# One decoder layer (gated linear attention and a convolutional FFN): FFN operand blocks moved to multiples of 256 bytes, bank evictions given an earlier place in the issue order, and side work placed on other units

## The chip, the cores and the metric

The kernel runs on one core of one Trainium2 chip. The metric is the device time of one execution in microseconds (us). Three timed executions of the kernel before took 2171.86, 2174.41 and 2174.84 us; their median, 2174.41 us, is the time before. A separate, profiled execution of the same kernel gave the trace that is read below.

## The reference, cut to what matters

One layer, sequence 2048, model width 1024, FFN width 2816, all in f32.

```python
def post_norm_residual(x, cs, w_mod, b_mod, ln_gain, ln_bias, sublayer):
    shift, scale, gate = jnp.split((cs @ w_mod + b_mod)[:, None, :], 3, axis=-1)
    y = sublayer(x * (1 + scale) + shift)
    return layer_norm(DN_ALPHA * x + (1 + gate) * y, ln_gain, ln_bias)

def gla_mixer(h, ...):                      # 4 heads, chunks of 64 tokens
    q, k, v, r, a_lr = split(h @ w_in)
    log_a = log_sigmoid(a_lr @ w_a2 + b_a) / 16      # the decays
    q_dec, k_inv, k_dec = q * exp(cumsum), k * exp(-cumsum), k * exp(last - cumsum)
    o = (causal part inside the chunk) + (state carried from chunk to chunk)
    return (rms_norm(o) * norm_g * silu(r)) @ w_o

def conv_ffn(h, w_up, conv_w, conv_b, w_down):
    u, g = split(h @ w_up)
    u = causal_conv_width_3(u) + conv_b
    return (silu(u) * g) @ w_down

x = post_norm_residual(x, ..., gla_mixer)
x = post_norm_residual(x, ..., conv_ffn)
```

## The kernel before, in words

**Products.** Every large product is made of 128x512 matmuls. An f32 operand is split into a rounded high part and a remainder (`split`, L104 on ScalarE and L107 on VectorE), and `mm3` (L110 to L112) issues high by high, high by low and low by high. Where a product has a 2x2 block form, it uses seven products in place of eight (the tuple `PROD` is their order); the sums that this needs are VectorE work.

**Stages, in order of time.** (1) A start with the modulation vectors and the first Q and K products. (2) `v_group(0)`, then `r_group(0)`: V, and R with its silu, for the first half of the tokens. (3) `v_group(1)` and `r_group(1)` for the second half. (4) The attention stage, seven segments of eight units each, in the order Q1, Q2, O0, Q3, O1, O2, O3 (`q_segment` makes Q and K of a block of 512 tokens, `o_segment` the output product of a block with the residual). The sixteen heads (four blocks by four heads) are worked in between. (5) The FFN's up product: 44 iterations (22 column blocks by two token halves) of seven products of 12 matmuls. Products 0, 1, 5 and 4 read their moving operand from tiles of tag `xa`, products 6, 3 and 2 from tiles of tag `xb`. (6) The down product with the last norm.

**Units and ticks.** A weight unit is one 512 KB block of a streamed weight (`unit`, `issue`, `load_unit`): it is loaded, split two units ahead of its use, and used by 24 matmuls. After a unit `tick()` runs the steps that are registered for it with `at_unit(u, f, ...)`. So the order in which side work stands in the program is written by hand as unit numbers: V0, R0, V1, R1, B0 = 0, 14, 34, 48, 68 are the first units of the stages, and B0 + 16, + 32, + 40, + 48 the first units of O0, O1, O2, O3. Side steps that matter here: `decays` (L564 on: a small matmul, then Identity, Abs, Exp, Ln on ScalarE, a scan on VectorE, two Exps; each call loads an activation table first), `x_prep` (loads and modulates x), `head_s`, `head_a`, `head_b`, `head_c`, `head_d` (the steps of a head), `ln1` and `normalise` (the first norm of 128 tokens: statistics on VectorE, the inverse root on GpSimd, the scaling on ScalarE), `ln1_out` (transposes the normed rows on TensorE into PSUM, L1305, and modulates them on VectorE, L1310), `load_z` (loads the rows of x to which O adds, L1319), `part_end` and `x_first` (free the attention tiles and make the FFN's first operands).

**Order on an engine.** All DMAs are issued by SyncE's queue. The framework sorts each engine's instructions at build time by a simulated run: of the instructions that the simulation finds ready, the one with the lowest number goes first, and the number is the place in the program. On the chip each engine then keeps that order. `tc.high_priority(offset=n)` lowers the numbers inside it by n; offset 0 leaves them as they are.

**Banks.** PSUM has two tags of four banks each. The big products use `mm`, the heads, transposes and decays mostly `w`. An eviction is the instruction that reads a finished bank: `keep` (L420, ScalarE) for the partial sums p1, u2 and u3; `qk_out` (L659, L660); the residual sum in `o_segment` (L1351, VectorE), which needs the rows from `load_z`; the product with `sr` in `head_d` (L1271); the split of `KTt` in `head_a`; the state update L1235 and the copy L1256.

**Addresses.** In the FFN stage a pool at the right end of SBUF holds, from the right: 224 bytes of constants, a 4096-byte tile `G`, two `U` tiles and eight `xa` tiles of 8192 bytes. A `U` tile is 1032 f32, 4128 bytes, so two take 8256 = 32*256 + 64 bytes and the `xa` tiles start at 192 modulo 256. The `xb` tiles and the weight tiles `hl` start at 0 modulo 256. In the down product both operands that are named `dhl` lie in `xa` tiles; one in three pairs lies in `hl` tiles.

Of the kernel before, what the change touches and what calls it, by code (L numbers as in the profile page):

```python
# [16 lines left out]
P = 128  # L17
# [21 lines left out]
def kernel(  # L39
# [84 lines left out]
    def load_unit():  # L124
        src = stream[len(stream_loads)][0]
        raw = src() if callable(src) else raw_tile()
        dst = raw if callable(src) or len(src.shape) == 2 else raw.rearrange("p (n x) -> p n x", n=4)
        stream_loads.append(None if callable(src) else load(dst, src))
        loaded.append(raw)

    def issue(n):
        while len(issued) < min(n, len(stream), stop[0]):
            src, keep_in, kept, gate = stream[len(issued)]
# [9 lines left out]
            if gate is not None:  # L143
                rv = raw.rearrange("p (k c) -> p k c", k=2)
                nc.vector.tensor_tensor(rv, rv, gate()[:, None, :].to_broadcast([P, 2, 512]), op=ALU.mult)
# [162 lines left out]
    def u_tile(up, name="U"):  # L308
        return up.tile([P, 1032], F32, tag="U", name=name, bufs=2)
# [69 lines left out]
    def at_unit(u, fn, *a):  # L379
        steps.setdefault(u, []).append((fn, a))  # L380

    def tick():
        u = pos[0]
        pos[0] += 1
        for fn, a in steps.pop(u, []):
            fn(*a)

# [30 lines left out]
    def keep(po, name):  # L418
        t = t2p.tile([P, 512], F32, tag="t2", name=name)
        return t, nc.scalar.copy(t, po)  # L420
# [5 lines left out]
    if True:  # L426
# [8 lines left out]
        h3_pool[0] = evp  # L435
        xrow = x.rearrange("(t p) d -> t p d", p=P)
# [123 lines left out]
        def a3_load(tb):  # L560
            a3[tb] = t2p.tile([P, TB], F32R, tag="t2", name="A3")[0:96]
            load(a3[tb].bitcast(F32), a3_d[tb])

        def decays(tb, heads):  # L564
# [3 lines left out]
            if "u3" in accs:  # L568
                order(ld, accs["u3"])
            A3 = a3.pop(tb)  # L570
            for h in heads:
# [21 lines left out]
                if tb < 2:  # L593
                    store(e_d[tb][h][:, lo], E1)
                    store(e_d[tb][h][:, hi], E2)

# [7 lines left out]
        def evac_a(pa, tb):  # L604
            A3 = t2p.tile([96, TB], F32R, tag="t2", name="A3")
            nc.scalar.copy(A3, pa[0:96])
            nc.vector.tensor_tensor(A3[32:64], pa[32:64], A3[32:64].bitcast(F32), op=ALU.subtract)
            store(a3_d[tb], A3.bitcast(F32))

# [47 lines left out]
        def qk_out(tb, h, pq, pk):  # L657
            t = raw_tile("qk")
            nc.scalar.copy(t[:, 0:512], pq)  # L659
            nc.scalar.copy(t[:, 512:1024], pk)  # L660
            store(qk_d[tb][h], t)

# [170 lines left out]
        def v_group(hf, X):  # L833
# [7 lines left out]
            for i in PROD:  # L841
# [76 lines left out]
        def x_stage1(i):  # L918
            raws = []
            for pr in range(2):  # L920
# [92 lines left out]
        def x_prep(pr):  # L1013
# [13 lines left out]
            store(xt1_d[3][pr], b21)  # L1027

# [18 lines left out]
        for k, f, pr in ((0, t_first, 1), (1, v_sums2, 0), (2, t_6, 0), (3, t_6, 1), (4, v_sums2, 1), (5, t_3, 0), (6, t_3, 1),  # L1047
                         (8, t_2, 0), (9, t_2, 1)):
            at_unit(V0 + k, f, pr)
        at_unit(V0 + 8, r_first, 0)  # L1050
        at_unit(V0 + 11, r_first1)
        at_unit(V0 + 12, r_first2)
        at_unit(V0 + 11, waw_load)
# [4 lines left out]
        at_unit(R0 + 3, x_prep, 0)  # L1058
        at_unit(R0 + 8, x_prep, 1)
# [4 lines left out]
        load(cb_sb, cb)  # L1064
        for n in range(16):
            u = V1 + 2 + n if n < 8 else R1 + n - 5
            at_unit(u, mods, n)
            if n % 4 == 3:
                at_unit(R1 + 2 if n < 8 else u + 2, mod_fin, 1, n // 4)
        at_unit(R1 + 14, mod2)  # L1070
        at_unit(V1 + 9, r_first, 1)
        at_unit(V1 + 11, r_first1)
        at_unit(V1 + 12, r_first2)
        at_unit(V1 + 11, waw_load)
        at_unit(R1, gate_rows, 2, XN1)
        at_unit(R1 + 4, waw_load)
        at_unit(R1 + 6, gate_rows, 3, XN1)
        for k in range(8):
            at_unit(R1 + 6 + k, gate_step, 0, k, gs1)
        at_unit(R1 + 17, gate_end, 0, gs1)  # L1080

        for pr in range(4):
            at_unit(R1 + 16, get_early, pr)
# [27 lines left out]
        def get(key, pr):  # L1111
            kind, tb = key
            t = xg_tile()
# [28 lines left out]
        def head_l(H):  # L1142
            tb, h = H["tb"], H["h"]
            if tb < 2:
                H["E"] = ab.tile([P, 2, 512], F32, tag="E", name="E")
                load(H["E"], e_d[tb][h].rearrange("p (s c) -> p s c", s=2))
            H["qk"] = ab.tile([P, 2, 512], F32, tag="qk", name="qk")
# [40 lines left out]
        def head_a(H):  # L1188
# [4 lines left out]
            split(KTt[:, 0], KTt[:, 1], pt)  # L1193
# [18 lines left out]
        def head_b(H):  # L1212
            h, v, KTt, el = H["h"], H["v"], H["KT"], H["el"]
            H["S"] = []
            for g in range(2):
# [9 lines left out]
                for i in range(2):  # L1225
# [6 lines left out]
                    if H["S"][s] is None:  # L1232
                        nc.vector.tensor_copy(new, po)
                    else:
                        nc.vector.scalar_tensor_tensor(new, old, el[:, 1, s:s + 1], po, op0=ALU.mult, op1=ALU.add)  # L1235
# [6 lines left out]
        def head_c(H):  # L1242
# [3 lines left out]
            for g in range(2):  # L1246
# [9 lines left out]
                nc.scalar.copy(on[:, 2 * g:2 * g + 2].rearrange("p s c -> p (s c)"), po)  # L1256
# [8 lines left out]
        def head_d(H):  # L1265
            on, sr = H["on"], H["sr"]
            for e in range(2):
# [3 lines left out]
                nc.vector.scalar_tensor_tensor(sr[:, e], pt, ng_sb[:, e:e + 1], sr[:, e], op0=ALU.mult, op1=ALU.mult)  # L1271
# [22 lines left out]
        def ln1_out(tb, zs, prs, by_act=False):  # L1294
            for pr in prs:
# [4 lines left out]
                for k in range(2):  # L1300
# [10 lines left out]
                    store(xm2_d[tb][pr][:, k], xt)  # L1311

# [21 lines left out]
        def o_segment(tb):  # L1334
            gated, zs = operand["O", tb], zs_of[tb]
            for half in range(2):
# [13 lines left out]
                for t in range(4):  # L1350
                    nc.vector.scalar_tensor_tensor(zs[t][:, cs_], zs[t][:, cs_], ALPHA, banks[t], op0=ALU.mult, op1=ALU.add)  # L1351
# [8 lines left out]
        def first_w():  # L1360
            first["W"] = w_load(0, 0)
            first["x"] = [raw_tile("xs") for pr in range(2)]

# [9 lines left out]
        def x_first(pr):  # L1373
            up, X0 = late_up["up"], late_up["X0"]
            tiles = {i: x_tile(up, i) for i in (0, 4, 5, 1)}
# [21 lines left out]
        head = []  # L1397
        for m in range(16):
            H = dict(tb=m // 4, h=m % 4, last=m // 4 == NTB - 1)
            head.append(H)  # L1400
            u = B0 + 1 + (11 * m) // 4
            if m >= 8:
                at_decays(u - 1, m // 4, (m % 4,))
            for k, f in ((-1, head_l), (0, head_s), (2, head_a), (2, head_v), (3, head_b), (6 if m in (2, 14) else 4, head_r), (5, head_c), (7, head_d)):
                at_unit(u + k, f, H)
        SEG = (("Q", 1), ("Q", 2), ("O", 0), ("Q", 3), ("O", 1), ("O", 2), ("O", 3))
        for n, key in enumerate(SEG):
            for pr in range(4):
                if n > 0:
                    at_unit(B0 + 8 * n - 4 + pr + {2: 1, 6: 2}.get(n, 0) * (pr == 3), get, key, pr)  # L1410
            if key[0] == "O":
                at_unit(B0 + 8 * n - 1, load_z, key[1])
# [443 lines left out]
```

## Time and profile before

| | us |
|---|---|
| median of three timed executions | 2174.41 |
| the profiled execution's own time | 2167.28 |
| its span in the trace | 2165.6 |
| TensorE (matmul) busy | 2119.0 (98%) |
| VectorE busy | 1566.5 (72%) |
| ScalarE busy | 1027.3 (47%) |
| GpSimd busy | 110.3 (5%) |

A group line of the profile reads: line, engine, operation, output <- inputs, shape, count | busy us, mean ns of one | idle us of the engine just ahead of them, and what ended it. A line of the waits reads: engine, what it was about to write, line <- what it waited for: us in total, times, longest. Matmul ends are modelled, so a mean of 389 ns is a duration and not the pace: matmuls overlap. A line of the table by stretches reads: window, its length, then busy us (count of instructions) of TensorE, its weight loads, VectorE, ScalarE and GpSimd, the granted TensorE clock, the DMA share and GB/s.

### The profile page before, as it was taken

The numbers are of one execution on the slowest core, as the hardware profiler recorded it, in microseconds if no ns is written. First come the engines' busy times: TensorE is split into PE (matmuls) and PEld (weight loads), VectorE is DVE, ScalarE is ACT, GpSimd is POOL, SyncE is SP. The second block draws the span as 40 slices with busy tenths as digits, with TensorE's granted clock in tenths as the row PEclk, the third lists the DMA queues.
The fourth block names the chain that finished last, engine by engine and source line by source line (L and its number), as shares of the span: only waits on it lengthen the run. The fifth ranks groups of instructions, "written<-read, shape, count | busy, mean of one in ns | idle before, by whom it ended". The sixth has DMA issues, their size and how long they took to land.

```text
span 2165.6 us, 27192 instructions
## 1 busy us (share of the span) xinstructions
PE 2119.0 (98%) x9741; PEld 1744.8 (81%) x9741; DVE 1566.5 (72%) x2143; ACT 1027.3 (47%) x1513; POOL 110.3 (5%) x250
## 2 busy tenths in 40 slices
PE   9999999999989999999999999999999999999998
PEld 7887788788878778788888887888888888888887
DVE  6856767677776865978777788666666797578557
ACT  4647735665666643544444454333333433344332
POOL 0000000001111101100000000000000000021001
PEclk9999999999999999999999999999999999999999
DMA  9778988878969778577855568868777797567662
GB/s 355 286 262 318 321 281 307 310 245 302 331 212 328 266 293 320 206 260 280 289 194 210 199 235 325 295 240 271 256 251 274 258 326 280 187 239 256 193 204 88
DMA packets 198839, 571.13 MB, mean 264 GB/s; under 512 B 24976, under 2 KB 41744, under 8 KB 188976
## 3 DMA queue, kind: packets, MB, share of 16 engines
q1 hardware_dynamic: 198704, 569.40, 75.0%
q8 instruction: 76, 1.25, 0.2%
q14 instruction: 59, 0.48, 0.1%
HBM read 378.61 MB, written 190.71 MB: 263 GB/s over the span
## 4 chain that ended last, share of the span: by engine, by line
PE 84%; ACT 4%; DVE 4%; DMA 4%; issue 2%; POOL 1%; SPq 0%; DVEq 0%; ACTq 0%; POOLq 0%
PE ps_mm L110 19%; PE ps_mm L111 19%; PE ps_mm L112 19%; PE ps_w L110 9%; PE ps_w L112 9%; PE ps_w L111 9%; DMA xp<-in_xT_dram 1%; DMA mraw<-in_mws_dram 1%; PE ps_w L1305 1%; ACT sq L1259 1%; ACT on L1262 1%; DMA raw<-in_wab_dram 1%; DMA v<-v_d 1%; PE ps_w L1270 0%; DVE az L585 0%
## 5 line engine op out<-in xcount | busy, mean ns | idle before, releaser
L110 PE MATMUL ps_mm<-xc,hl 128*128 128x512 f32 x856 | 338.2, 395 | 7.0 <-ACT p L420 5.3
L111 PE MATMUL ps_mm<-xc,hl 128*128 128x512 f32 x856 | 337.2, 394 | 0.0
L112 PE MATMUL ps_mm<-xc,hl 128*128 128x512 f32 x856 | 335.7, 393 | 0.0
L110 PEld LDWEIGHTS ps_mm<-xc,hl 128*128 128x128 f32 x856 | 160.7, 188 | 48.2 <-ACT p L420 7.4
L112 PEld LDWEIGHTS ps_mm<-xc,hl 128*128 128x128 f32 x856 | 160.8, 188 | 37.7 <-DVE hl L107 0.2
L111 PEld LDWEIGHTS ps_mm<-xc,hl 128*128 128x128 f32 x856 | 160.8, 188 | 37.0 <-issue 0.2
L112 PE MATMUL ps_w<-xc,hl 128*128 128x512 f32 x432 | 169.6, 393 | 2.0 <-DVE hl L107 2.0
L111 PE MATMUL ps_w<-xc,hl 128*128 128x512 f32 x432 | 170.1, 394 | 0.0
L110 PE MATMUL ps_w<-xc,hl 128*128 128x512 f32 x432 | 170.1, 394 | 0.0
L420 ACT COPY u<-ps_mm 128x512 f32<-128x512 f32 x104 | 60.7, 584 | 191.1 <-PE ps_mm L112 188.4
L1453 DVE SCALAR_TENSOR_TENSOR ct<-U,cw_sb,ct 128x512 f32<-128x512 f32 x176 | 131.6, 747 | 24.1 <-ACT ct L1447 21.6
L107 DVE TENSOR_TENSOR hl<-raw,hl 128x1024 fp32r<-128x1024 f32 (+1 forms) x87 | 98.4, 1134 | 55.5 <-ACT hl L104 55.0
L104 ACT CAST dhl<-raw 128x1024 fp32r<-128x1024 f32 x57 | 59.7, 1047 | 158.1 <-PE ps_mm L112 97.2
L104 ACT CAST hl<-wu 128x1024 fp32r<-128x1024 f32 x82 | 86.0, 1049 | 101.7 <-PE ps_mm L112 66.2
L104 ACT CAST hl<-raw 128x1024 fp32r<-128x1024 f32 (+1 forms) x87 | 84.9, 980 | 93.1 <-PE ps_mm L112 40.4
L107 DVE TENSOR_TENSOR hl<-wu,hl 128x1024 fp32r<-128x1024 f32 x82 | 100.2, 1223 | 32.9 <-ACT hl L104 32.9
L107 DVE TENSOR_TENSOR dhl<-raw,dhl 128x1024 fp32r<-128x1024 f32 x57 | 69.5, 1219 | 66.8 <-ACT dhl L104 66.8
L110 PE MATMUL ps_mm<-hl,xg 128*128 128x512 f32 x256 | 102.9, 402 | 5.3 <-DVE zs L1351 3.9
L111 PE MATMUL ps_mm<-dhl 128*128 128x512 f32 x264 | 102.8, 389 | 0.0
L112 PE MATMUL ps_mm<-dhl 128*128 128x512 f32 x264 | 102.8, 389 | 0.0
L110 PE MATMUL ps_mm<-dhl 128*128 128x512 f32 x264 | 102.7, 389 | 0.0
L112 PE MATMUL ps_mm<-hl,xg 128*128 128x512 f32 x256 | 101.9, 398 | 0.0
(295 smaller groups left out, 5084.2 us busy)
## 6 DMA issues: line engine op xcount, KB each, us to landing
hc_d<-ct SPq DMA_DIRECT2D x154, 256.0 KB, 2.8
raw<-hc_d SPq DMA_DIRECT2D x70, 512.0 KB, 4.3
draw<-wc_d SPq DMA_DIRECT2D x70, 512.0 KB, 4.7
raw<-in_wab_dram SPq DMA_DIRECT2D x48, 512.0 KB, 6.0
hl<-wq_d SPq DMA_DIRECT2D x24, 1024.0 KB, 7.0
wu<-in_wup_dram SPq DMA_DIRECT2D x44, 512.0 KB, 5.4
wg<-in_wup_dram SPq DMA_DIRECT2D x44, 512.0 KB, 4.3
wh_d<-hl SPq DMA_DIRECT2D x22, 1024.0 KB, 4.8
```

The source lines that it names most:

```text
L104: accs["copy"] = nc.scalar.copy(h, src)
L107: return nc.vector.tensor_tensor(l, src if lsrc is None else lsrc, h.bitcast(F32), op=ALU.subtract)
L110: nc.tensor.matmul(po, a[0], b[0], start=first, stop=False, skip_group_check=resumed)
L111: nc.tensor.matmul(po, a[0], b[1], start=False, stop=False, skip_group_check=resumed)
L112: return nc.tensor.matmul(po, a[1], b[0], start=False, stop=last, skip_group_check=resumed)
L420: return t, nc.scalar.copy(t, po)
L1259: nc.scalar.activation(sq, on[:, s], AF.Square, scale=1.0 / 16.0, accum_out=ss[:, s:s + 1])
L1262: nc.scalar.activation(on[:, s], on[:, s], AF.Copy, scale=ss[:, s:s + 1])
L1305: nc.tensor.transpose(pt[:, t * P:t * P + P], src, ident)
L1453: nc.vector.scalar_tensor_tensor(ct, U[:, o + i:o + i + 512], cw_sb[:, j, i:i + 1], ct, op0=ALU.mult, op1=ALU.add)
```

## The change

It does four things. The `U` tile grows from 1032 to 1056 f32 (4224 bytes; two are 33*256), which moves the `xa` tiles by 192 bytes to 0 modulo 256. Evictions are wrapped in `high_priority`: `keep` by 300, the residual sums by 300, the products with `sr` by 1200, the split of `KTt` by 60, the V copies by 600, and with offset 0 `qk_out`, the state update and the copy `on`. `ln1` leaves `o_segment` and becomes a step of its own, and many unit numbers change. The product of the O weights with the gate moves from `issue` to `load_unit`, and two of these units are loaded earlier.

```diff
     def load_unit():
+        gate = stream[len(stream_loads)][3]
         stream_loads.append(None if callable(src) else load(dst, src))
+        if gate is not None:
+            rv = raw.rearrange("p (k c) -> p k c", k=2)
+            nc.vector.tensor_tensor(rv, rv, gate()[:, None, :].to_broadcast([P, 2, 512]), op=ALU.mult)
         loaded.append(raw)
...
     def u_tile(up, name="U"):
-        return up.tile([P, 1032], F32, tag="U", name=name, bufs=2)
+        return up.tile([P, 1056], F32, tag="U", name=name, bufs=2)
...
     def keep(po, name):
         t = t2p.tile([P, 512], F32, tag="t2", name=name)
-        return t, nc.scalar.copy(t, po)
+        with tc.high_priority(offset=300):
+            return t, nc.scalar.copy(t, po)
...
     # v_group
-                        nc.scalar.copy(dst, A[t])
+                        with tc.high_priority(offset=600):
+                            nc.scalar.copy(dst, A[t])
...
-        for u, heads in ((4, (0,)), (9, (1,)), (14, (2, 3))):
-            at_decays(R0 + u, 0, heads)
-            at_decays(R1 + u, 1, heads)
+        D_AT = (17, 20, 24, 27, 51, 54, 58, 62)
+        for m, u in enumerate(D_AT):
+            at_decays(u, m // 4, (m % 4,))
-        at_unit(R0, gate_rows, 1, X)
-        at_unit(R1, gate_rows, 2, XN1)
-        at_unit(R1 + 6, gate_rows, 3, XN1)
+        GR_AT = (17, 49, 56)
...
     # head_a; head_d
-            split(KTt[:, 0], KTt[:, 1], pt)
+            with tc.high_priority(offset=60):
+                split(KTt[:, 0], KTt[:, 1], pt)
...
-                nc.vector.scalar_tensor_tensor(sr[:, e], pt, ng_sb[:, e:e + 1], sr[:, e], op0=ALU.mult, op1=ALU.mult)
+                with tc.high_priority(offset=1200):
+                    nc.vector.scalar_tensor_tensor(sr[:, e], pt, ng_sb[:, e:e + 1], sr[:, e], op0=ALU.mult, op1=ALU.mult)
...
     # o_segment
-                for t in range(4):
-                    nc.vector.scalar_tensor_tensor(zs[t][:, cs_], zs[t][:, cs_], ALPHA, banks[t], op0=ALU.mult, op1=ALU.add)
-                    if half == 1 and tb < NTB - 1:
-                        ln1(tb, t, zs)
+                with tc.high_priority(offset=300):
+                    for t in range(4):
+                        nc.vector.scalar_tensor_tensor(zs[t][:, cs_], zs[t][:, cs_], ALPHA, banks[t],
+                                                       op0=ALU.mult, op1=ALU.add)
                 tick()
-                if half == 0 and tb == NTB - 1:
-                    part_end()
...
-        for tb, u in ((0, 24), (1, 40), (2, 48)):
-            at_unit(B0 + u + 1, lambda tb: ln1_out(tb, zs_of[tb], range(0, 2)), tb)
-            at_unit(B0 + u + 2, lambda tb: ln1_out(tb, zs_of[tb], range(2, 4)), tb)
-        at_unit(B0 + 49, first_w)
-        at_unit(B0 + 53, x_first, 1)
-        at_unit(B0 + 53, lambda: (w_sums1(first["W"]), w_h0(first["W"])))
-        at_unit(B0 + 54, lambda: (w_sums2(first["W"]), w_h2(first["W"])))
+        LN_AT = ((23, 23, 24, 24, 26, 26, 27, 27), (39, 39, 40, 40, 42, 42, 43, 43), (47, 47, 48, 48, 49, 49, 50, 50))
+        for tb in range(3):
+            for t in range(4):
+                at_unit(B0 + LN_AT[tb][t], lambda tb, t: ln1(tb, t, zs_of[tb]), tb, t)
+                at_unit(B0 + LN_AT[tb][4 + t], lambda tb, t: ln1_out(tb, zs_of[tb], (t,), BY_ACT[tb][t]), tb, t)
+        LU_AT = (14.9, 14.95)
+        for u in LU_AT:
+            at_unit(B0 + u, load_unit)
+        F_AT = (49, 50, 52, 54, 55)
+        for u, f, a in zip(F_AT, (first_w, part_end, x_first, first_w1, first_w2), ((), (), (1,), (), ())):
+            at_unit(B0 + u, f, *a)
```

`BY_ACT` is all zero, so `ln1_out` stays on VectorE. `tick` now sorts its steps by their number, which may have a fraction. The head steps keep their units; the rest of the diff moves single steps by a fraction of a unit or by one, and `assert` lines check the order.

More of the change, by code (lines that the diff above doesn't have):

```diff
@@ L1 @@
+import math
 from contextlib import ExitStack
@@ L132, in issue @@
         while len(issued) < min(n, len(stream), stop[0]):
-            src, keep_in, kept, gate = stream[len(issued)]
+            src, keep_in, kept, _ = stream[len(issued)]
             if kept is not None:
@@ L384, in tick @@
         pos[0] += 1
-        for fn, a in steps.pop(u, []):
+        for _, fn, a in sorted(steps.pop(u, []), key=lambda s: s[0]):
             fn(*a)
@@ L435 @@
         h3_pool[0] = evp
+        made = set()
         xrow = x.rearrange("(t p) d -> t p d", p=P)
@@ L560, in a3_load @@
         def a3_load(tb):
+            assert ("a", tb) in made
             a3[tb] = t2p.tile([P, TB], F32R, tag="t2", name="A3")[0:96]
@@ L569, in decays @@
                 order(ld, accs["u3"])
+            assert ("a", tb) in made
             A3 = a3.pop(tb)
@@ L595, in decays @@
                     store(e_d[tb][h][:, hi], E2)
+                made.add(("E", tb, h))
         def mm_a(pa, w, xs, kts):
@@ L608, in evac_a @@
             store(a3_d[tb], A3.bitcast(F32))
+            made.add(("a", tb))
         def waw_load():
@@ L658, in qk_out @@
             t = raw_tile("qk")
-            nc.scalar.copy(t[:, 0:512], pq)
-            nc.scalar.copy(t[:, 512:1024], pk)
+            with tc.high_priority(offset=0):
+                nc.scalar.copy(t[:, 0:512], pq)
+                nc.scalar.copy(t[:, 512:1024], pk)
             store(qk_d[tb][h], t)
+            made.add(("qk", tb, h))
         X = [None] * 7
@@ L919, in x_stage1 @@
             raws = []
+            assert ("xp", 0) in made and ("xp", 1) in made
             for pr in range(2):
@@ L1027, in x_prep @@
             store(xt1_d[3][pr], b21)
+            made.add(("xp", pr))
         gs1 = {}
@@ L1112, in get @@
             kind, tb = key
+            assert kind == "Q" or ("g", tb, pr) in made
             t = xg_tile()
@@ L1146, in head_l @@
                 load(H["E"], e_d[tb][h].rearrange("p (s c) -> p s c", s=2))
+            assert ("qk", tb, h) in made and (tb >= 2 or ("E", tb, h) in made)
             H["qk"] = ab.tile([P, 2, 512], F32, tag="qk", name="qk")
@@ L1231, in head_b @@
                     new = S32[:, h] if i == 1 else t2p.tile([P, DV], F32, tag="t2", name="S1")
[L1232 to L1235, printed above, removed]
+                    with tc.high_priority(offset=0):
+                        if H["S"][s] is None:
+                            nc.vector.tensor_copy(new, po)
+                        else:
+                            nc.vector.scalar_tensor_tensor(new, old, el[:, 1, s:s + 1], po, op0=ALU.mult, op1=ALU.add)
                     st1 = ab.tile([P, 2, DV], F32R, tag="Shl", name="Shl", bufs=8)
@@ L1255, in head_c @@
                         mm3(pos_, (Q[:, 0, s, 0:128], Q[:, 1, s, 0:128]), (st[:, 0], st[:, 1]), False, True)
-                nc.scalar.copy(on[:, 2 * g:2 * g + 2].rearrange("p s c -> p (s c)"), po)
+                with tc.high_priority(offset=0):
+                    nc.scalar.copy(on[:, 2 * g:2 * g + 2].rearrange("p s c -> p (s c)"), po)
             sq = t2p.tile([P, DV], F32, tag="t2", name="sq")
@@ L1311, in ln1_out @@
                     store(xm2_d[tb][pr][:, k], xt)
+                made.add(("x", tb, pr))
         zs_of = {}
@@ L1362, in first_w, with first_w1, first_w2 @@
             first["x"] = [raw_tile("xs") for pr in range(2)]
+        def first_w1():
+            w_sums1(first["W"])
+            w_h0(first["W"])
+        def first_w2():
+            w_sums2(first["W"])
+            w_h2(first["W"])
         late_up = {}
@@ L1374, in x_first @@
             up, X0 = late_up["up"], late_up["X0"]
+            assert all(("x", b, p) in made for b in range(2) for p in (pr, 2 + pr))
             tiles = {i: x_tile(up, i) for i in (0, 4, 5, 1)}
@@ L1395, in x_first @@
                     X0[i].append((t[:, 0, k * 512:k * 512 + 512], t[:, 1, k * 512:k * 512 + 512]))
-        head = []
+        H_AT = (1, 3, 6, 9, 12, 14, 17, 20, 23, 25, 28, 31, 34, 36, 39, 42)
+        D2_AT = (22, 24, 27, 30.5, 33, 35, 38, 41)
+        STEP = (-1, 0, 2, 2, 3, 4, 5, 7)
         for m in range(16):
             H = dict(tb=m // 4, h=m % 4, last=m // 4 == NTB - 1)
-            head.append(H)
-            u = B0 + 1 + (11 * m) // 4
+            u = B0 + H_AT[m]
             if m >= 8:
-                at_decays(u - 1, m // 4, (m % 4,))
-            for k, f in ((-1, head_l), (0, head_s), (2, head_a), (2, head_v), (3, head_b), (6 if m in (2, 14) else 4, head_r), (5, head_c), (7, head_d)):
+                at_decays(B0 + D2_AT[m - 8], m // 4, (m % 4,))
+            for k, f in zip(STEP, (head_l, head_s, head_a, head_v, head_b, head_r, head_c, head_d)):
+                if f is head_r and m in (2, 14):
+                    k = 6.5
@@ L1405 @@
                 at_unit(u + k, f, H)
         SEG = (("Q", 1), ("Q", 2), ("O", 0), ("Q", 3), ("O", 1), ("O", 2), ("O", 3))
-        for n, key in enumerate(SEG):
+        GET = ((4, 5, 6, 7), (12, 13, 14, 16), (20, 21, 22, 23), (28, 29, 30, 31), (36, 37, 38, 39), (44, 45, 46, 49))
+        for n, key in enumerate(SEG[1:]):
             for pr in range(4):
[L1409 to L1412, printed above, removed]
@@ L1413 @@
[L1413 to L1419 removed]
+                at_unit(B0 + GET[n][pr], get, key, pr)
```

59 lines of the change are left out of this document (33 added, 26 removed).

## The prediction

> **What bounds the kernel now.** I read the page first, then the table of busy time by stretches, then the waits of TensorE, and last short windows around single waits.
>
> ```profile
> span 2165.6 us, 27192 instructions
> PE 2119.0 (98%) x9741; PEld 1744.8 (81%) x9741; DVE 1566.5 (72%) x2143; ACT 1027.3 (47%) x1513; POOL 110.3 (5%) x250
> ```
>
> TensorE is busy for 98% of the span, the next engine, VectorE, for 72%. So time can go in two ways only: a matmul gets shorter, or TensorE's idle time does. The stretches say where each is to be had.
>
> ```profile
> core 0: us, PE busy (x) PEld busy (x) DVE busy (x) ACT busy (x) POOL busy (x), PEclk, DMA share, GB/s
> 148.00:220.00 72.00, 66.23 (x289) 53.10 (x287) 43.95 (x53) 54.14 (x75) 0.00 (x0) 1.00 0.86 308
> ...
> 311.00:400.00 89.00, 88.00 (x398) 70.70 (x396) 65.87 (x91) 52.10 (x72) 0.00 (x0) 1.00 0.88 302
> 523.00:680.00 157.00, 142.49 (x788) 122.59 (x786) 118.52 (x204) 97.22 (x196) 21.23 (x39) 0.96 0.80 290
> 680.00:872.00 192.00, 182.51 (x970) 155.88 (x971) 131.29 (x224) 96.78 (x189) 22.72 (x51) 0.97 0.79 288
> 872.00:895.00 23.00, 20.58 (x80) 15.72 (x79) 21.56 (x24) 12.41 (x15) 0.20 (x2) 0.93 0.51 173
> 900.00:1300.00 400.00, 400.00 (x1749) 324.46 (x1748) 313.13 (x423) 180.42 (x244) 14.49 (x52) 1.00 0.69 240
> 1310.00:1720.00 410.00, 410.00 (x1775) 331.96 (x1774) 280.32 (x368) 144.09 (x196) 7.14 (x22) 1.00 0.79 270
> 1735.00:2150.00 415.00, 415.00 (x1825) 342.36 (x1824) 288.94 (x352) 165.73 (x188) 30.47 (x48) 1.00 0.67 226
> ```
>
> The R products of the first half (148 to 220) leave TensorE idle for 72.00 - 66.23 = 5.8 us, the attention stage from 523 on for 14.5 and 9.5, the start of the FFN for 2.4. The FFN and the down product leave nothing. But their pace differs: 410 / 1775 = 231.0 ns a matmul in the FFN, 415 / 1825 = 227.4 in the down product, though both are 128x512 matmuls at the full clock (1.00). The waits name what ends the idle time:
>
> ```profile
> PE ps_mm L110 <- DVE zs L1351: 5.8, 3, 3.9
> PE ps_mm L110 <- ACT p L420: 5.3, 4, 3.6
> PE ps_w L1305 <- DVE KTt L107: 4.1, 2, 3.0
> PE ps_w L1305 <- ACT mn L577: 2.9, 1, 2.9
> PE ps_w L110 <- DVE sr L1271: 2.8, 1, 2.8
> PE ps_w L110 <- DMA v<-v_d: 2.3, 1, 2.3
> PE ps_mm L110 <- ACT qk L659: 2.2, 2, 1.4
> PE ps_w L110 <- ACT on L1256: 2.1, 2, 1.9
> PE ps_w L112 <- DVE hl L107: 2.0, 1, 2.0
> ...
> PE ps_mm L110 <- ACT u L420: 1.6, 1, 1.6
> ```
>
> Most are late evictions: a bank is finished, and the engine that should empty it is at other work.
>
> **Part 1, the FFN operands at 0 modulo 256.** Two products of one FFN iteration, 12 matmuls each, first product 2 (moving operand in an `xb` tile, at 0), then product 4 (in an `xa` tile, at 192):
>
> ```profile
> L111 PE MATMUL ps_w<-xc,hl 128*128 128x512 f32 x4 | 1.6, 392 | 0.0
> L110 PE MATMUL ps_w<-xc,hl 128*128 128x512 f32 x4 | 1.6, 390 | 0.0
> L112 PE MATMUL ps_w<-xc,hl 128*128 128x512 f32 x4 | 1.6, 389 | 0.0
> ```
> ```profile
> L112 PE MATMUL ps_w<-xc,hl 128*128 128x512 f32 x5 | 2.0, 393 | 0.0
> L110 PE MATMUL ps_w<-xc,hl 128*128 128x512 f32 x4 | 1.6, 394 | 0.0
> L111 PE MATMUL ps_w<-xc,hl 128*128 128x512 f32 x4 | 1.6, 394 | 0.0
> ```
>
> (In the second window one of the five in the first row belongs to the next product.) At 192 all take 394 ns; at 0 they take 389 to 392. TensorE has no idle time there, so each ns counts. The `xa` products are 4 x 12 x 44 = 2112 matmuls. At 394 - 389 = 5 ns this gives 10.6 us. The low end takes the mean of the three rows at 0, 390.3: 3.7 ns, 7.8 us. The high end lets the whole FFN (7 x 12 x 44 = 3696 matmuls) reach the down product's pace: 3.59 ns, 13.3 us. I take 10.6.
>
> The Trainium skill's page "SBUF — State Buffer", section "Door 1: The DMA port swizzle", gives SBUF lines of 16 bytes, and a penalty only where an access crosses to a new line; 192 is 12 such lines, so by that rule alone the shift is worth 0 and the sum below would be 10.6 us smaller. The rows at 192 and 0 speak against it.
>
> The down product's `dhl` operands move too, both of them. The four rows that bound this:
>
> ```profile
> L111 PE MATMUL ps_mm<-dhl 128*128 128x512 f32 x264 | 102.8, 389 | 0.0
> ...
> L111 PE MATMUL ps_mm<-hl,xc 128*128 128x512 f32 x128 | 49.8, 389 | 0.0
> ...
> L110 PE MATMUL ps_mm<-hl 128*128 128x512 f32 x88 | 34.5, 392 | 0.0
> ...
> L111 PE MATMUL ps_mm<-hl 128*128 128x512 f32 x88 | 34.2, 389 | 0.0
> ```
>
> With both operands at 192 they take 389, the least that any such row shows, so nothing is gained. At 0 and 0 the V products (`hl,xc`) also take 389, while pairs of `hl` take 392 on two of three lines. So 0 to 2 ns on 1368 matmuls, 0 to 2.7 us lost. I take 0, by the 389 of the V products, which have as many tiles in turn.
>
> **Part 2, evictions.** In the first R stage TensorE's longest wait for p1 ends with this on ScalarE:
>
> ```profile
> 212.66 1.28 ACT L565 ACT_TABLE_LOAD   x1
> ...
> 214.49 0.67 ACT L577 ACTIVATE mn<-ps_w,ba_sb 128x512 f32<-128x512 f32 x1
> ...
> 219.62 0.58 ACT L420 COPY p<-ps_mm 128x512 f32<-128x512 f32 x1
> ```
>
> The copy that frees the bank stands behind two heads of decays that one step had put there. Now each step has one head, and the copy has priority 300. The whole row of p1 goes: 5.3. The 1.6 for u2 stays, since ahead of that copy ScalarE itself waits for a load of x, and an order can't cure that. The price: two more table loads (eight calls in place of six, 1.28 each); ScalarE is busy 54 of 72 us in that stage, so it hides them. Without that cover they cost 2.6.
>
> The residual sums: two of their three waits come from the norm's statistics put between the four sums, the longest from VectorE's backlog of head work. The statistics leave and the sums get priority 300: 5.8 goes. The product with `sr` waited behind a gate product whose weight was landing; it now has priority 1200 and the gate product comes with an earlier load: 2.8 goes. `KTt` and `mn` (7.0) end waits of the transposes in `ln1_out`, where these meet `head_a`, `head_c` and, after unit 41, decays. Of block 1 they move to units 42 and 43, away from both (4.0 of the 7.0); of block 0 to 26 and 27, where `head_a` is met again (half of 3.0): 5.5 goes. The FFN's first operands are made from unit 50 and 52 on in place of 51 and 53, so the 2.0 for `hl` at the first up product goes. What is late next in each place is the following matmul's own weights, whose split is done two units ahead. `qk`, `on` and the state update have offset 0, which changes no place: 2.2 and 2.1 stay, and so does the load of `v`.
>
> **Part 3, what the change adds.** The residual rows of O2 need the four tiles of block 1 back, and these are free only after the last transposes of `ln1_out`. Before:
>
> ```profile
> 787.16 1.16 PE L1305 MATMUL ps_w<-ident,zs 128*128 128x128 f32 x8
> ...
> 793.84 0.40 PE L110 MATMUL ps_mm<-hl,xg 128*128 128x512 f32 x1
> ```
> ```profile
> 788.03 1.76 SPq L1319 DMA_DIRECT2D zs<-in_x_dram  x4
> ```
> ```profile
> 794.94 0.69 DVE L1351 SCALAR_TENSOR_TENSOR zs<-zs,ps_mm 128x512 f32<-128x512 f32 x1 [0.78 <-DMA zs<-in_x_dram]
> ```
>
> The last transposes are done at 788.1, SyncE issues the four loads at 788.0, VectorE already waits 0.78 us for the third, and TensorE takes the freed bank at 793.84. That just fits. Now the last transposes stand after unit 43, whose 24 matmuls take 24 x 0.227 = 5.5 us. The loads go out that much later, the sums wait on VectorE with the splits for later units behind them, and TensorE's unit 44 waits for its bank. Between 0 (the build's order finds head work to fill it) and 8 (5.5 and half as much again for the last tiles); I take 5. The four loads also stand in SyncE's queue ahead of weight loads; those have two units of cover, about 11 us of matmuls.
>
> **The sum**, on the profiled execution (2167.28 us): -10.6 (FFN) - 5.3 (p1) - 5.8 (residual sums) - 2.8 (`sr`) - 5.5 (transposes) - 2.0 (`hl`) + 5 (O2) = -27.0, so 2140.3. The median of the timed runs lies 7.1 us above the profiled run; the same 27.0 from 2174.41 gives **2147.4**.
>
> **The rivals.** *The waits move and don't go:* each of these engines is full around the segments (VectorE is busy 118.5 of 157 us and waits for ScalarE in between), so an eviction that goes first makes a split or a transpose late by as much, and only the FFN pays: 2174.4 - 10.6 = 2163.8, with the O2 wait 2168.8. For it: the waits in the attention stage have nine different causes, which points at load more than at order. Against it: the two largest groups lose work that stood inside them. *The 256 bytes do nothing*, and the 5 ns come from another trait of these tiles: 2147.4 + 10.6 = 2158.0. Against it: `xb` and `xa` differ in nothing else that the code shows. *Slower:* in the FFN, `keep` gets in front of convolution and split work in every iteration.
>
> ```profile
> L420 ACT COPY u<-ps_mm 128x512 f32<-128x512 f32 x104 | 60.7, 584 | 191.1 <-PE ps_mm L112 188.4
> ...
> L104 ACT CAST hl<-wu 128x1024 fp32r<-128x1024 f32 x82 | 86.0, 1049 | 101.7 <-PE ps_mm L112 66.2
> ```
>
> If two copies of 0.584 us make the weight cast late in each of 44 iterations, that is 51.4 us: 2147.4 + 51.4 = 2198.8. It decides from the point where the casts end less than 0.6 to 1.2 us ahead of their matmuls. Against it: ScalarE's casts wait for TensorE to free the tile (66.2 us in all), not the other way about, and ScalarE is busy 180 of 400 us there.
>
> **How the numbers follow.** About 0.2% (4.3 us) can be told from no change. The forecast has 0.68, waits that move 0.17, no effect of the address 0.09, slower 0.06. The forecast's own bounds: at best 13.3 in the FFN and all idle time of TensorE in the five stretches above (5.8 + 1.0 + 14.5 + 9.5 + 2.4 = 33.2), 46.5 us: 2128. At worst 7.8 in the FFN, 2.7 lost in the down product, half of the 21.4 us of waits, and 8 for O2: a gain of 7.8, 2167. That reaches into the case of moved waits too; left out are the slower case, half of the moved waits and the forecast's tails, about 0.19. Faster by over 0.2% (below 2170.1) takes the forecast, the address case and nearly all moved waits: 0.91. Within 0.2%: 0.03. Slower: 0.06.
>
> **What would show it.** In the changed profile: the FFN stretches at 228 to 229 ns a matmul, and 389 to 391 ns for both kinds of products; the rows of p1, `zs` and `sr` gone from the waits or under 1 us each; a new wait for `zs` or for its load where O2 goes from its first half to its second; `qk`, `on` and `v` about as before. It is wrong if FFN matmuls on `xa` still show 394, if the idle time between 523 and 872 stays above 20 us, or if the FFN shows waits of TensorE for splits.

## The result and the profile after

| | before | after |
|---|---|---|
| median of the timed executions, us | 2173.14 (4) | 2151.91 (4) |
| ratio, 95% interval | | 0.9905 (0.9883 to 0.9927) |
| profiled execution's own time, us | 2167.28 | 2154.09 |
| span in the trace, us | 2165.6 | 2151.4 |

The change saves 21.2 us where 27.0 were forecast; 2151.91 lies inside the range, 4.5 us above the number. The page of the kernel after:

```profile
span 2151.4 us, 27162 instructions
...
PE 2103.0 (98%) x9741; PEld 1747.5 (81%) x9741; DVE 1565.6 (73%) x2143; ACT 1042.9 (48%) x1523; POOL 109.6 (5%) x250
```

TensorE is busy for 16.0 us less (2119.0 - 2103.0) with the same 9741 matmuls: the matmuls got shorter. Its idle time rose a little, from 2165.6 - 2119.0 = 46.6 to 48.4 us. The busy time by stretches of the kernel after shows where; the columns are those of the table of before, and the last stretch ends 10 us earlier, because the kernel ends earlier:

```profile
148.00:220.00 72.00, 67.68 (x289) 54.05 (x288) 41.74 (x51) 58.97 (x77) 0.00 (x0) 0.98 0.79 292
...
523.00:680.00 157.00, 143.23 (x793) 123.98 (x792) 119.17 (x208) 96.24 (x198) 20.04 (x39) 0.96 0.80 287
680.00:872.00 192.00, 177.87 (x954) 150.94 (x953) 128.83 (x222) 97.76 (x191) 22.80 (x51) 0.98 0.81 295
872.00:895.00 23.00, 21.27 (x93) 16.99 (x92) 20.94 (x25) 12.59 (x14) 0.20 (x2) 1.00 0.44 148
...
1310.00:1720.00 410.00, 410.00 (x1811) 339.48 (x1809) 284.83 (x374) 151.77 (x206) 7.12 (x22) 1.00 0.79 274
1735.00:2140.00 405.00, 405.00 (x1788) 335.47 (x1787) 281.13 (x343) 162.72 (x185) 30.48 (x48) 1.00 0.66 222
```

In the FFN 1811 matmuls fit into 410 us in place of 1775: 226.4 ns each, before 231.0. The down product went from 227.4 to 405 / 1788 = 226.5. The idle time from 523 to 872 is 13.8 + 14.1 = 27.9 us, before 24.0. So the gain lies in the pace of the matmuls, and the order of the work saved no idle time. The waits of TensorE in the kernel after (engine, tile, line, what it waited for: us in total, times, longest):

```profile
PE ps_w L111 <- DVE sr L1292: 6.0, 2, 5.5
PE ps_w L111 <- ACT on L1276: 5.9, 3, 5.3
PE ps_w L1327 <- DVE S L1254: 5.6, 1, 5.6
PE ps_mm L111 <- ACT u L422: 4.3, 2, 3.0
PE ps_mm L111 <- DVE zs L1375: 4.2, 3, 2.1
PE ps_w L111 <- ACT hl L105: 2.9, 2, 1.9
PE ps_mm L111 <- ACT qk L667: 2.2, 2, 1.4
PE ps_mm L111 <- ACT hl L105: 1.7, 1, 1.7
...
PE ps_w L111 <- DMA v<-v_d: 1.2, 1, 1.2
```

The ten rows quoted for before sum to 31.1 us, these nine to 34.0. `p`, `KTt` and `mn` are gone; `on`, `u`, `sr` and `hl` grew, and `S` is new in the list. Three of them (`S`, `sr`, `on`) hold a single wait of over 5 us.

### The profile page after: what moved, and what is told of

It reads as the page before. It is cut to its first block, busy times and chain, and to the rows that moved or that the text cites. A ratio compares the mean times of both kernels' runs of the same rounds, so it can differ in the third digit from the quotient of the medians.

```text
span 2151.4 us, 27162 instructions
## 1 busy us (share of the span) xinstructions
PE 2103.0 (98%) x9741; PEld 1747.5 (81%) x9741; DVE 1565.6 (73%) x2143; ACT 1042.9 (48%) x1523; POOL 109.6 (5%) x250
## 4 chain that ended last, share of the span: by engine, by line
PE 82%; DVE 5%; DMA 5%; ACT 5%; issue 2%; POOL 1%; SPq 0%; DVEq 0%; ACTq 0%; POOLq 0%
PE ps_mm L111 18%; PE ps_mm L113 18%; PE ps_mm L112 18%; PE ps_w L111 8%; PE ps_w L112 8%; PE ps_w L113 8%; DMA raw<-in_wab_dram 1%; ACT hl L105 1%; DMA mraw<-in_mws_dram 1%; PE ps_mm L491 1%; PE ps_w L750 1%; PE ps_w L1327 1%; DVE xc L108 1%; DMA qk<-qk_d 1%; DMA v<-v_d 0%
## 5 line engine op out<-in xcount | busy, mean ns | idle before, releaser
L111 PE MATMUL ps_w<-xc,hl 128*128 128x512 f32 x432 | 168.4, 390 | 1.1 <-ACT hl L105 1.0
L113 PE MATMUL ps_w<-xc,hl 128*128 128x512 f32 x432 | 168.2, 389 | 0.3 <-DVE hl L108 0.3
L112 PE MATMUL ps_w<-xc,hl 128*128 128x512 f32 x432 | 168.1, 389 | 0.0
```

Of the source, the lines that this page charges most:

```text
L111: nc.tensor.matmul(po, a[0], b[0], start=first, stop=False, skip_group_check=resumed)
L112: nc.tensor.matmul(po, a[0], b[1], start=False, stop=False, skip_group_check=resumed)
L113: return nc.tensor.matmul(po, a[1], b[0], start=False, stop=last, skip_group_check=resumed)
```

## The experiments

In the first two, A is the theory that the address paid everything and the order nothing; B is the forecast's split.

**1. The address alone.**

```diff
 # kernel before
-        return up.tile([P, 1032], F32, tag="U", name=name, bufs=2)
+        return up.tile([P, 1056], F32, tag="U", name=name, bufs=2)
```

> The kernel before with the U tile at 1056 in place of 1032 elements a row, and nothing else of the change: only the xa and dhl operands move from 192 to 0 modulo 256 bytes. Theory A (the address pays everything and the order of the work nothing): ratio to before 0.9915 to 0.9925, some 17 to 18 us less, FFN at 226.4 to 227.5 ns a matmul for xa and xb alike, waits as before. Theory B (the forecast's split, 10.6 us by the address and about as much by the order): ratio about 0.995, some 10.6 us less, the FFN at 228 to 229 ns.

2154.18 us against 2172.87: ratio 0.9915 (0.9901 to 0.9930), 18.7 us less, as A says. The same FFN stretch (us, TensorE busy and matmuls, clock, DMA share, GB/s):

```profile
1310.00:1720.00 410.00, 410.00 (x1811) 1.00 0.79 275
```

1811 matmuls, as in the kernel after. By the pace the effect is (231.0 - 226.4) x 3696 = 17.0 us in the FFN, and (227.4 - 226.5) x 1848 = 1.7 us in the down product (1368 matmuls on `dhl`, 480 on `hl`), in sum 18.7. That this meets the difference of the medians so exactly is partly chance. In the two traces the FFN, from its first matmul to the first of the down product, took 859.1 and 842.9 us, and the down product 425.2 and 423.5, in sum 17.9 us less; the stages ahead of them took 4.8 us longer in this execution, which had 6.8 us more at half the granted clock there.

**2. The order alone.** The kernel after with 1032 in place of 1056.

> The kernel after with the U tile back at 1032 elements: all of the new order, none of the new addresses. Theory A: ratio to before 0.998 to 1.002 (0 +- 4 us), with the FFN at 231 ns a matmul and waits of TensorE between 523 and 872 as many as before. Theory B: ratio 0.992 to 0.995, 11 to 17 us less than before.

2170.52 us, ratio 0.9991 (0.9981 to 1.0001): 2.4 us less, which can't be told from nothing (the interval holds 1). A again. Its longest waits are those of the kernel after (on 5.3, S 5.6, sr 4.7).

**3 and 4. Other offsets.** The kernel before with 1040 (`xa` and `dhl` at 128) and with 1048 elements (at 64).

> The kernel before with the U tile at 1040 elements: xa and dhl at 128 modulo 256 bytes, the other operands at 0. Theory 'only multiples of 256 count': ratio 0.998 to 1.002, FFN matmuls with xa at 394 ns. Theory 'a multiple of 128 is enough': ratio about 0.992, 389 ns. Theory '16-byte lines, the address doesn't matter and something else of the tile does': ratio 1.000 too, but then the run with 1056 elements shows 1.000 as well.

> The kernel before with the U tile at 1048 elements: xa and dhl at 64 modulo 256 bytes (1048 x 4 = 4192, the next tile starts 32 bytes on where the allocator pads to 32). Theory 'only multiples of 256 count' or 'every offset that differs from that of the other operand costs the same': ratio 0.998 to 1.002, 394 ns. Theory 'what counts is the distance from a 256-byte boundary': between before and the run at 128, a third of the 5 ns. Theory 'a multiple of 64 is enough': ratio about 0.992, but then 192 would not have cost anything, so this is against the trace of before.

Ratios 0.9985 (0.9973 to 0.9996) and 0.9984 (0.9971 to 0.9998): neither 128 nor 64 is enough. At 64 the cost is spread in another way. The groups of the FFN in that kernel:

```profile
L110 PE MATMUL ps_mm<-xc,hl 128*128 128x512 f32 x663 | 262.5, 396 | 0.0
L112 PE MATMUL ps_mm<-xc,hl 128*128 128x512 f32 x664 | 260.7, 393 | 0.0
L111 PE MATMUL ps_mm<-xc,hl 128*128 128x512 f32 x663 | 258.2, 389 | 0.0
```

Of the three matmuls that make one product the first takes 396 ns and the second 389; at 192 all three took 393 or 394. The pace comes out nearly the same: 1783 matmuls in 410 us, 229.9 ns each, where before had 231.0. That is 4 us over the FFN, about what the ratio shows.

**5. All operands at 192.** An unused tile of 192 bytes ahead of the pools on the left:

```diff
 # kernel before
+    const.tile([P, 48], F32, name="shift")
     smp = ctx.enter_context(tc.tile_pool(name="smp", bufs=6))
```

> The kernel before (U tile of 1032 elements, old order) with one unused tile of 192 bytes ahead of the pools on the left side, so that the weights (hl), xb, xg and h3 move to 192 modulo 256 too: in the FFN and the down product all operands then lie at 192, none at 0. Theory 'each operand must lie at 0 modulo 256': nothing gets faster, ratio 0.999 to 1.003, FFN at 231 ns a matmul or more. Theory 'operands must lie alike, at whatever offset' (a mix of offsets costs, not the offset): the FFN at 226.4 to 227.5 ns a matmul and the down product at 226.7, as in the run that moved xa and dhl to 0, ratio 0.991 to 0.994, with some us lost where operands of the first stages that stay at 0 (the second x pool, Q, v) now meet weights at 192.

2158.59 us, ratio 0.9933 (0.9918 to 0.9947): 14.1 us less, with no FFN matmul operand at 0 by the sizes of the tiles. Its FFN stretch:

```profile
1310.00:1720.00 410.00, 410.00 (x1810) 1.00 0.79 275
```

226.5 ns a matmul, so what counts is that the operands lie alike. The reverse shows in the first half, where weights now at 192 meet an x pool that stayed at 0. The V products there, before and in this kernel:

```profile
L111 PE MATMUL ps_mm<-hl,xc 128*128 128x512 f32 x128 | 49.8, 389 | 0.0
```
```profile
L112 PE MATMUL ps_mm<-hl,xc 128*128 128x512 f32 x128 | 50.2, 392 | 0.0
```

Here a shift away from a common offset made the same matmuls 3 ns longer.

**6 and 7. Priorities alone, moved steps alone,** both with the new addresses. The first is experiment 1 with the five `high_priority` wraps that are not 0, every step at its old unit; the second is the kernel after with these five set to 0:

```diff
 # 6: experiment 1
+        with tc.high_priority(offset=300):      # keep; likewise p1 600, KTt 60, sr 1200, zs 300
+            return t, nc.scalar.copy(t, po)
 # 7: kernel after
-        with tc.high_priority(offset=300):
+        with tc.high_priority(offset=0):
```

> The new addresses and the raised priorities alone (kept copies 300, p1 copies 600, KTt 60, sr 1200, residual sums 300), every step at its old unit; the norm's statistics stay between the residual sums. Theory 'the waits move and don't go': the same as the run with the addresses alone, ratio 0.990 to 0.993. Theory of the forecast (priority frees the banks, p1 and zs): some 5 to 8 us less than the addresses alone, ratio 0.988 or below, with p1 and zs gone from the waits of TensorE. Third: the moved steps, not the priorities, cost what came back (S, sr, on): then this is faster than the whole change, ratio 0.987 to 0.989.

> The kernel after with all raised priorities set to offset 0: the new addresses and the moved steps alone. 'The waits move': ratio 0.990 to 0.993. 'The moved steps cost what the priorities gain': slower than the addresses alone by 4 to 8 us, ratio 0.994 to 0.996, with p1 and zs back among the waits beside S, sr and on.

Experiment 6: 2166.41 us, ratio 0.9968 (0.9958 to 0.9978), by the ratios 11.5 us slower than the addresses alone, which none of the three expectations gave. Experiment 7: 2154.98 us, 0.9923 (0.9910 to 0.9937), the same as the addresses alone. In 6 the evictions did go earlier: `p` waits fell from 5.3 to 3.5 and `zs` from 5.8 to 4.2. But TensorE's idle time rose from 2152.5 - 2105.0 = 47.5 (addresses alone) to 2161.7 - 2106.9 = 54.8 us, and two waits for weights are new:

```profile
PE ps_w L110 <- ACT hl L104: 4.9, 1, 4.9
...
PE ps_mm L110 <- ACT hl L104: 2.5, 2, 2.4
```

ScalarE near 237 us, in the run with the addresses alone and then in this one:

```profile
237.42 1.99 ACT L104 CAST hl<-raw 128x1024 fp32r<-128x1024 f32 x2
```
```profile
236.54 1.03 ACT L104 CAST hl<-raw 128x1024 fp32r<-128x1024 f32 x1
...
250.37 1.04 ACT L104 CAST hl<-raw 128x1024 fp32r<-128x1024 f32 x1 [2.50 <-DMA raw<-in_wab_dram]
```

There two weights are cast by 239.4. Here only one is. The load of the other stands later in SyncE's queue. In the run with the addresses alone it went out at 223.29, here only together with the next one:

```profile
243.33 1.97 SPq L128 DMA_DIRECT2D raw<-in_wab_dram  x2
```

So its cast comes at 250.37, and TensorE, done at 246.6, waits for it. This is near the rival "the waits move", since a split becomes late, but the split is late by its load and not by an eviction ahead of it on ScalarE. That the raised priorities moved the load in the build's order follows from the edit, which has nothing else in it; how they did is not shown. Beside the moved steps (experiment 7 against the kernel after) the same priorities cost nothing.

**8. The gate product at its old place,** in `issue` in place of `load_unit`, in the kernel after.

> The kernel after with the gate product back at its old place, in the step that splits the weight, in place of the step that loads it. Theory 'the gate product stands ahead of sr on VectorE and waits for its weight's landing': TensorE's wait for sr at 533 us, 5.6 us in the kernel after, falls to 3 or less, and the time by some 3 us to a ratio of 0.988 to 0.990. Theory 'the wait has the landing of qk behind it and the gate product only fills it': the wait stays at 5 to 6 us, and the ratio at 0.9905.

2153.81 us, 0.9912 (0.9896 to 0.9928). The wait for `sr` fell to 2.0, as the first theory says, but the time didn't: a wait of 2.6 for `v` appeared at 550. VectorE in the kernel after shows why `sr` was late, though its priority is 1200:

```profile
534.94 0.43 DVE L1178 SCALAR_TENSOR_TENSOR Q<-qk,E 128x256 f32<-128x256 f32 x1 [4.46 <-DMA qk<-qk_d]
...
537.35 1.23 DVE L133 TENSOR_TENSOR raw<-raw,G 128x1024 f32<-128x1024 f32 x1 [0.79 <-DMA raw<-in_wab_dram]
538.50 1.40 DVE L1292 SCALAR_TENSOR_TENSOR sr<-ps_w,ng_sb,sr 128x512 f32<-128x512 f32 x2
```

Two instructions that wait for DMAs, 4.46 and 0.79 us, stand ahead of it. VectorE keeps the order of the build, and the priority didn't bring `sr` ahead of them. The likely reason is that the build plans from estimated times and not from the landings; its plan is not on record.

**9. Block 1's transposes one unit earlier,** where before had them.

```diff
 # kernel after, LN_AT[1]
-(39, 39, 40, 40, 42, 42, 43, 43)
+(39, 39, 40, 40, 41, 41, 42, 42)
```

> The kernel after with the last two transposed pairs of block 1's norm one unit earlier (41 and 42, where before had them, in place of 42 and 43). Forecast: the wait for zs where O2 goes from its first to its second half (2.3 us in the kernel after, 5 in the forecast) falls below 1 us, and waits of the transposes for KTt or mn (4.0 us in before) come back. Theory 'the transposes meet decays or head work wherever they stand, one wait replaces another': the wait of 5.8 us for S ends or moves, a wait of 3 to 6 us for another tile stands in its place, and the ratio stays at 0.989 to 0.992. If instead S alone was the price of the move: ratio 0.987 to 0.988.

2149.92 us, 0.9888 (0.9871 to 0.9905). Its waits:

```profile
PE ps_mm L111 <- DVE zs L1375: 3.9, 3, 1.8
...
PE ps_w L1327 <- ACT mn L582: 3.4, 1, 3.4
```

The wait for `S` of 5.6 is gone (one of 1.6 is left elsewhere) and `mn` (3.4) is back, as the second theory says. The ratio is a little below its range, but its interval overlaps that of the kernel after, so no gain is shown. The wait at O2 stays at 1.8, where less than 1 was forecast, though the transposes are back at their place.

**10. Priority 300 for `on` and `S`,** 0 in the kernel after.

> The kernel after with the copies of on and the updates of S at priority 300 in place of 0. Theory 'an eviction late because of its place in the engine's order is cured by priority': the waits for on (5.9 us) and S (5.6 us) fall below 2 us each and the time by 5 to 9 us, ratio 0.986 to 0.988. Theory 'the order is planned from estimated times, in which on and S aren't ready yet when the work ahead of them is put down; priority moves nothing that the plan sees as not ready': S stays at 5 to 6 us, on changes by 2 us at most, ratio 0.989 to 0.992.

2154.10 us, 0.9909 (0.9893 to 0.9924), and the waits:

```profile
PE ps_w L111 <- ACT on L1276: 8.9, 4, 5.6
PE ps_w L1327 <- DVE S L1254: 5.6, 1, 5.6
```

Neither wait got shorter, so the first theory is out. The second fits for `S`, whose neighbours on VectorE come in the same order as in the kernel after. For `on` it allowed 2 us of change, and the sum rose by 3.0, with 4 waits in place of 3. That a priority only chooses among what the planned run sees as ready is the likely reading; the plan itself is not on record.

**11 and 12. Work in the waits.** Experiment 9 with 40 matmuls that add zeros to a running bank, put ahead of the wait for `on` (11), and ahead of the wait for `sr` too (12):

```diff
 # experiment 9, head_a, between the two groups of P; KEEP = {(2, 0): 40}, in 12 also (1, 1): 40
+                for _ in range(KEEP.get((H["tb"], H["h"]), 0) if g == 0 else 0):
+                    held = nc.tensor.matmul(run[0][:, 0:P], zero, still[:, 0:P], start=False, stop=False, skip_group_check=True)
+                    order(held, mm)
+                    mm = held
```

> The kernel of the run before (block 1's norm one unit earlier) with 40 matmuls of 128x128 that add zeros to a running sum, put on TensorE right ahead of the matmul that waits 5.3 us for on near 614 us; the order on the other engines stays the same but for one place of VectorE. In the profiles so far each wait of 3 us or more is followed by 3.5 or 7 us at half the granted clock, which loses 1.71 or 3.41 us more. Theory 'a long wait costs twice, once itself and once by the clock that the idle time takes away': the matmuls fill the wait (about 4.4 us of its 5.3), the granted clock stays at 1.00 from 612 to 630, and the time falls by 3.4 us, ratio 0.986 to 0.988. Theory 'the half clock has another cause than the idle time (the load of the chip, or a rhythm of its own)': the clock falls as before, ratio 0.988 to 0.990. If the zeros take longer than the wait: slower by up to 2 us.

> As the run with zeros ahead of the wait for on, and the same 40 zero matmuls ahead of the wait for sr near 532 us too (5.4 us, and 3.41 us of half clock behind it). There the plan of the other engines' order changes with it (gate products earlier, residual sums and sr two places apart). If the second wait stays where it is and is filled: no half clock near 537, 3.4 us less than the run with one, ratio 0.986 to 0.988. If the changed order moves the wait to another place, or the zeros stand in front of ready work: no gain or up to 4 us lost, ratio 0.989 to 0.991.

The stretches around the wait for `on`, in experiment 9 and then in 11 (columns as above; the third number from the end is the granted clock):

```profile
612.00:617.00 5.00, 1.95 (x16) 1.60 (x14) 3.85 (x6) 3.19 (x5) 2.75 (x3) 1.00 0.83 314
617.00:622.00 5.00, 2.10 (x8) 2.00 (x9) 3.50 (x5) 4.40 (x9) 0.77 (x2) 0.61 0.60 188
622.00:627.00 5.00, 5.00 (x17) 3.92 (x17) 4.93 (x11) 3.71 (x12) 1.68 (x3) 0.71 0.82 274
```
```profile
612.00:617.00 5.00, 4.33 (x39) 4.16 (x38) 4.78 (x8) 3.71 (x5) 2.38 (x3) 1.00 0.83 306
617.00:622.00 5.00, 4.12 (x35) 3.94 (x35) 2.56 (x3) 3.79 (x6) 0.47 (x2) 1.00 0.58 205
622.00:627.00 5.00, 5.00 (x24) 4.12 (x23) 4.95 (x11) 4.66 (x15) 1.58 (x4) 1.00 0.96 306
```

In 9 the clock falls to 0.61 and 0.71, which loses (0.39 + 0.29) x 5 = 3.4 us. In 11 it stays at 1.00, and 24 matmuls pass from 622 to 627 in place of 17. So here the idle time is what takes the clock away. Part of the gain is lost again to a wait of 2.2 for `S` right behind it. The time, 2147.91 us, is 2.0 us below experiment 9, but the ratio, 0.9889 (0.9869 to 0.9908), is that of experiment 9 (0.9888): the 3.4 us of the forecast don't show in the time. Nor does its sentence that 3.5 or 7 us at half clock follow each long wait hold throughout: 10.2 us follow the wait of 5.3 for `on` in experiment 8, and none the wait of 3.1 for `u` at 170 in this run.

Experiment 12 took 2153.40 us, 0.9910 (0.9894 to 0.9925). The wait for `sr` was filled as intended, to 0.5 us, and the granted clock stayed at 1.00 from 532 to 547, which repeats the finding of 11. But other waits came behind it, with 10.2 us at half clock from 550 on; the longest is this one:

```profile
555.47 0.58 PE L111 MATMUL ps_w<-v,KTt 128*128 128x256 f32 x1 [4.09 <-DMA v<-v_d]
```

## Why the prediction was right in its number and wrong in its split

That the number came out near is luck, by two errors of opposite sign: the address was forecast at 10.6 and gave 18.7, the order at 16.4 and gave 2.4 (experiment 2), or 2.3 (the kernel after against experiment 1), neither of which can be told from nothing.

**Address, 10.6.** That the address pays was right, the size and the account of where were wrong. I counted only the 2112 matmuls whose own operand moved, and took the 389 to 392 ns of the `xb` products as what a matmul at 0 costs. Those too were slowed by the mix. With all operands alike the groups of the FFN are at 389 and 390:

```profile
L111 PE MATMUL ps_mm<-xc,hl 128*128 128x512 f32 x679 | 264.9, 390 | 0.0
L112 PE MATMUL ps_mm<-xc,hl 128*128 128x512 f32 x680 | 264.5, 389 | 0.0
```

Even the high end, 13.3, was too low. It took the down product's 227.4 ns for the floor, where `dhl` at 192 and `hl` at 0 were mixed as well; `hl` pairs fell from 392 to 389 there, which the forecast had put down as a possible loss for `dhl`. So the down product, put at 0, gained 1.7 us. A difference of durations (5 ns of 394) was also the wrong measure: the pace of the stretch, 4.6 ns on 3696 matmuls, had all of it (226.4 where 228 to 229 were expected). By the rule of 16-byte lines on the Trainium skill's page "SBUF — State Buffer", section "Door 1: The DMA port swizzle", a shift of 192 bytes would be worth 0; experiment 1 measured 18.7 us, so this rule alone doesn't cover the case. The rival that the 256 bytes do nothing is out.

**p1, 5.3.** Gone from the list. But `u` rose from 1.6 to 4.3, so 2.6 was saved. The longest `u` wait (3.0 us) ends with this copy, which itself waits for VectorE:

```profile
169.15 0.59 ACT L422 COPY u<-ps_mm 128x512 f32<-128x512 f32 x1 [1.09 <-DVE h L108]
```

VectorE makes that `h` behind two differences of `x_prep` (L1030, from 166.03 to 168.51), a step that stands at unit 17 in both kernels. A priority on ScalarE can't reach them.

The added table loads show no price: the stage's idle time fell from 5.8 to 72.00 - 67.68 = 4.3.

**Residual sums, 5.8, and O2, +5.** 5.8 became 4.2, 2.1 of it at O2's change of halves, the wait that was forecast there. VectorE waits for the loads, for the first of the four sums here and again, 1.94 us, for the second at 802.26, with which TensorE's wait ends:

```profile
798.31 0.69 DVE L1375 SCALAR_TENSOR_TENSOR zs<-zs,ps_mm 128x512 f32<-128x512 f32 x1 [2.66 <-DMA zs<-in_x_dram]
```

The place was right, the cause is not shown: in experiment 9 the wait stays at 1.8 with the transposes at their old unit, and in 10 it is 0.7 with them at the new one. What makes the loads land late is open.

**`sr`, 2.8.** Wrong: it rose to 6.0. Priority 1200 didn't bring it ahead of two instructions that wait for DMAs. One is the gate product, which moved to the load, but its weight had not landed there either (experiment 8).

**Transposes, 5.5 of 7.0.** `KTt` and `mn` went and `S` came with 5.6: 1.4 saved. Away from `head_a` and `head_c`, the transposes met `head_b`, whose state update (the last row) stands behind a decay chain on VectorE that itself waits for ScalarE:

```profile
778.81 0.69 DVE L589 TENSOR_TENSOR mn<-mn,az 128x512 f32<-128x512 f32 x1 [2.14 <-ACT az L588]
779.54 1.23 DVE L590 TENSOR_TENSOR_SCAN az<-smask,mn 128x512 f32<-128x512 f32 x1
...
781.92 0.48 DVE L1254 SCALAR_TENSOR_TENSOR S<-S,el,ps_w 128x256 f32<-128x256 f32 x1
```

**`hl` at the FFN's start, 2.0.** 1.7 stays. Elsewhere the forecast took the splits, made two units ahead, as in time, and so it had no term for weights; in the kernel after TensorE waits 1.0 us for `hl` at 226 and 1.9 us at 254, where before it didn't. **`qk`** as forecast, 2.2. **`v`** fell from 2.3 to 1.2, and **`on`**, which an offset of 0 was to leave alone, rose from 2.1 to 5.9: ahead of it on ScalarE there now stands a scaling of `normalise` at 619.19, a moved step, which waits 1.78 us for GpSimd. An offset of 0 keeps a place in the program, but not what its neighbours wait for.

Of the rivals, "the waits move and don't go" described the order part in its outcome. Of the forecast's own signs, the idle time between 523 and 872 stayed above 20 us, which it had named as a sign of being wrong. "Slower" didn't come: past the FFN's start no wait for splits appears (399.94 of 400 us busy from 900 to 1300); one such wait, 2.4 us, shows in experiment 6.

## What to carry to other kernels

Let all operands that TensorE reads in one stretch start alike modulo 256 bytes, and judge it by the pace of the stretch, not by the duration of single groups. Before counting a wait as saved, ask what the waiting engine has next and which DMA that needs: here a raised priority cured neither `sr` nor `on` nor `S`, and the waits that went were replaced by others of about the same sum. Count the clock that a wait can take away with the wait itself.

## What the runs showed of the hardware

**Mixed offsets.** With moving operands at 192, 128 or 64 modulo 256 among others at 0, TensorE's pace in the FFN was 231.0, 230.7 or 229.9 ns a matmul; with all at 0 or all at 192, 226.4 or 226.5. In the down product pairs with both operands at 0 (`hl`) took 392 ns on two of three lines while pairs at 192 ran among them, and 389 with all at 0; the `dhl` pairs took 389 to 390 at 192 and 389 at 0. Why is not shown, nor whether the moving or the stationary operand decides. The offsets are counted from the sizes of the tiles; no trace prints an address.

**A wait can be paid twice.** The stretches of the kernel after around its wait for `sr` (granted clock third from the end):

```profile
533.00:537.00 4.00, 0.84 (x8) 0.67 (x6) 1.52 (x4) 0.00 (x0) 0.04 (x1) 1.00 1.04 425
537.00:541.00 4.00, 1.70 (x7) 1.71 (x8) 3.65 (x5) 2.39 (x3) 0.00 (x0) 0.74 0.75 302
541.00:545.00 4.00, 4.00 (x10) 3.05 (x10) 3.90 (x9) 0.81 (x3) 0.00 (x0) 0.50 0.73 282
545.00:549.00 4.00, 4.00 (x19) 3.31 (x18) 4.00 (x5) 1.35 (x3) 0.00 (x0) 0.90 0.64 243
```

After 5.5 us of idle time the clock is lower for (0.26 + 0.50 + 0.10) x 4 = 3.4 us of lost work, more than half of the wait again. A busy share hides this, since TensorE counts as busy at half speed: 10 matmuls in 541 to 545. The loss does not follow the length of the wait alone. In the kernel before the wait for `sr`, which ends at 534.7, has 2.8 us and costs as much, (0.47 + 0.38) x 4 = 3.4 us:

```profile
534.00:538.00 4.00, 3.32 (x11) 2.94 (x12) 3.96 (x7) 2.76 (x4) 0.00 (x0) 0.53 0.67 285
538.00:542.00 4.00, 4.00 (x13) 3.15 (x12) 3.94 (x7) 1.19 (x3) 0.00 (x0) 0.62 0.95 280
```

The span and mean granted clock of the kernel, before and after:

```profile
core 0: 2165.6 us, clock 0.992
```
```profile
core 0: 2151.4 us, clock 0.992
```

0.008 x 2165.6 is 17 us in either, so the change gave back nothing here, and the forecast had no term for it. The Trainium skill's page "TensorE: Matmul & The Clock Gate", section "Part 1: The HAM clock gate", describes a gate at half rate that follows windows of about 3.4 us of activity; the 0.50 of the third row of the kernel after agrees. Experiments 11 and 12 show at one wait each that it is the idle time that lowers the clock.
